# Retention and mLSTM: score-value products in plain fp32 instead of three fp32r matmuls on split operands

## The chip, the cores and the metric

The kernel runs on one core of one Trainium2 chip. The metric is the device time of one execution in microseconds; three runs of the kernel before gave 1383.99 (median), 1382.55 and 1386.01.

## The reference

A backbone of two layers works on 256 latent and 256 context tokens of width 1024. Layer 0 has a Mamba-2 (SSD) head group, four retention heads (query and key width 128, value width 256), an output projection and a SwiGLU FFN; layer 1 has an mLSTM block with four heads of width 512, its output projection and a second FFN; a last RMSNorm follows. The change touches one line of each mixer. In `decay_scan`, which retention uses:

```
scores = jnp.einsum('bihd,bjhd->bijh', qc, kc) * decay
y = (jnp.einsum('bijh,bjhe->bihe', scores, vc) + ...)
```

and in `mlstm_scan`:

```
s = jnp.einsum('bihd,bjhd->bijh', qc, kc) * jnp.exp(d - m_out[:, :, None, :])
num = (jnp.einsum('bijh,bjhe->bihe', s, vc) + ...)
```

The kernel computes both scans without chunks: all weighted scores of a head at once, forward and backward together, and then one product of scores and values.

## The kernel before, in words

All tokens stand side by side as 512 columns or four chunks of 128 rows. Each large product is done in split form: an fp32 operand is cast to a high part H of type fp32r, the rest L = x - H is kept in fp32r too, and `mm3` (L403) sums H·H, H·L and L·H in three fp32r matmuls (L407 to L409). Weights come through a list `plan` of 512 KB tiles: SP loads them (`wload`, L351), ScalarE casts wH (L367) and VectorE, for a few tiles named in `on_pool` POOL, subtracts wL (L368; the trace books every `tensor_tensor` on the helper's line L227).

Layer 0 takes its units in the order of `UNITS` (L378): R is a retention head, G an SSD group, O a quarter of the output projection. A retention head projects queries, keys, gate and values (`ret_proj`, L889); `projB` hands each of four 128 x 256 value blocks to `ev`, which copies it to vt (L905) and subtracts its low part vl (L906). `ret_scan` runs beside it as a background generator. It makes the decay matrix dm (L936), six score blocks in three PSUM tiles by plain fp32 matmuls (L945, L950), and hands each PSUM tile to `ret_split`: a product with dm on VectorE (L929), a cast on ScalarE (L931), a subtraction on POOL (L932), all of tiles named pT. Then come twelve pairs of a 128 x 128 score block and a 128 x 256 value block through `mm3` (L963), and the norm.

Layer 1 is driven by a string `order` (L1431): z is a tile of the z projection, c a step of the gate chain, h0 to h3 a step of a head's generator `ml_head` (L1312), d a tile of the down projection. A head's first step loads the decay rows ur (urow), splits its four value chunks into vH on ScalarE (L1319) and vL on POOL (L1320), and for each of two row blocks computes on VectorE and ScalarE the arguments of the exponentials (earg: L1329, L1331), their product with the scores (L1332), the divisor (rr) and the sum of both directions (L1342). The second step transposes the result on TensorE (L1349), copies it out of PSUM as pH (L1352) and subtracts pL on VectorE (L1353). The third makes eight pairs of a 128 x 128 block and a 128 x 512 value chunk through `mm3` (L1359) and the norm (L1362 to L1368); the fourth transposes back (L1376) and writes the operands of the down projection.

The tile framework allots the rotating buffers (tag s2: 36 of 2 KB per partition; tag s4: 8 of 4 KB), sets all semaphores and lays down, when the kernel is built, the order of each engine's instructions; SP alone keeps the order of the program. So the matmuls of a z tile can stand before and after a transpose of a head.

Of the kernel before, what the change touches and what calls it, by code (L numbers as in the profile page):

```python
# [17 lines left out]
P = 128  # L18
# [168 lines left out]
def tile_hybrid(ctx, tc, A, out, dbg=None):  # L187
# [35 lines left out]
    def f32v(t):  # L223
        return t.bitcast(F32)
# [664 lines left out]
    def ret_proj(h, pre=None):  # L889
        ready = {}  # L890
        bg.add(ret_scan(h, ready), True)

        def pa():
            p = projA(hs)
            slot()
            return p
        qk = ret_qk((pa, pa)) if pre is None else pre
        vt = pool[0].tile([P, NCH, 256], F32R, tag="s4", name=nm("vt"), bufs=8)
        gs = s4("gs")
        projB(hs, lambda c, p: S.activation(gs[:, c, :], p, AF.Silu))  # L900
        ready["qk"] = qk
        vl = [s2("vl", (P, 2, 256), F32R) for _ in range(2)]

        def ev(c, p):
            S.copy(out=vt[:, c, :], in_=p)  # L905
            tt(V, vl[c // 2][:, c % 2, :], p, f32v(vt)[:, c, :], ALU.subtract)  # L906
        projB(hs, ev)
        ready["vg"] = (vt, vl, gs)

    def ret_decay(h):  # L910

# [11 lines left out]
        tt(G, dm[:, 3, 128:256], ef[:, 0:128], eb[:, 384:512], ALU.add)  # L923
        return dm

    def ret_split(p, dm):

        t = s2("pT", (P, 2, 256))
        tt(V, t, p, dm, ALU.mult)  # L929
        H, L = (s2("pT", (P, 2, 256), F32R) for _ in range(2))  # L930
        S.copy(out=H, in_=t)  # L931
        tt(G, L, t, f32v(H), ALU.subtract)  # L932
        return [(H[:, j, :], L[:, j, :]) for j in range(2)]

    def ret_scan(h, ready):
        dm = ret_decay(h)  # L936
        yield
        while "qk" not in ready:
            yield
        q, k = ready["qk"]  # L940
        pt = []
        for jj in range(2):
            p = scps([P, 2, 256])
            for j in range(2):
                TE.matmul(p[:, j, :], lhsT=k[:, (jj * 2 + j) * P:(jj * 2 + j + 1) * P], rhs=q[:, LT_],  # L945
                          start=True, stop=True)
            pt += ret_split(p, dm[:, jj * 2:jj * 2 + 2, :])
        p = scps([P, 2, 256])
        for j in range(2):
            TE.matmul(p[:, j, :], lhsT=k[:, j * P:(j + 1) * P], rhs=q[:, CT_], start=True, stop=True)  # L950
        tc_ = ret_split(p, dm[:, 2:4, :])
        yield
        while "vg" not in ready:
            yield
        vt, vl, gs = ready["vg"]
        mv = small("mv", [P, NCH, 2], 2)
        rs = small("rsr", [P, NCH], 2)
        y = s4("yret")
        for st in range(2):
            py = scps([P, 2, 256])  # L960
            srcs = tc_ if st == 0 else pt
            for i in range(2):
                mm3(py[:, i, :], [(cols(src, slice(i * P, (i + 1) * P)), (vt[:, j, :], vl[j // 2][:, j % 2, :]))  # L963
                                  for j, src in enumerate(srcs)])
            sl = slice(st * 2, st * 2 + 2)
            for i in range(2):
                bs = small("bs", [P, 6], 2)
                V.bn_stats(out=bs, in_=py[:, i, :])
                V.bn_aggr(out=mv[:, st * 2 + i, :], in_=bs)
            V.tensor_scalar(out=rs[:, sl], in0=mv[:, sl, 1], scalar1=LN_EPS, scalar2=None, op0=ALU.add)  # L970
            tt(G, rs[:, sl], rs[:, sl], mhalf[:, :2], ALU.pow)
            for i in range(2):
                c = st * 2 + i
                V.scalar_tensor_tensor(out=y[:, c, :], in0=py[:, i, :], scalar=mv[:, c, 0:1], in1=gs[:, c, :],
                                       op0=ALU.subtract, op1=ALU.mult)
            for c in (st * 2, st * 2 + 1):
                S.activation(y[:, c, :], y[:, c, :], AF.Copy, scale=rs[:, c:c + 1])
            yield
        yield
        to_feat(y, (8 + 2 * h, 9 + 2 * h), (None, None))  # L980
        yield
# [330 lines left out]
    def ml_head(h):  # L1312
        ur = [s2x("urow") for _ in range(2)]
        for d in range(2):
            nc.sync.dma_start(out=ur[d], in_=scr2[d, h, :].partition_broadcast(P))
        vhl = []
        for c in range(NCH):
            H, L, v = s2("vH", dt=F32R), s2("vL", dt=F32R), vts[h][:, c, :]
            S.copy(out=H, in_=v)  # L1319
            tt(G, L, v, f32v(H), ALU.subtract)  # L1320
            vhl.append((H, L))
        pms = []
        for it in range(2):
            negm = small("negm", [P, 2], 2)
# [21 lines left out]
        for it in range(2):  # L1346
            pp = scps([P, NCH, P])
            for c in range(NCH):
                TE.transpose(pp[:, c, :], pms[it][:, c * P:(c + 1) * P], ident)  # L1349
            pp = pp.rearrange("p a b -> p (a b)")  # L1350
            H, L = s2("pH", dt=F32R), s2("pL", dt=F32R)
            S.copy(out=H, in_=pp)  # L1352
            tt(V, L, pp, f32v(H), ALU.subtract)  # L1353
            pts.append((H, L))
        yield
        ys = []
        for it in range(2):
            py = scps()
            mm3(py, [(cols(pts[it], slice(c * P, (c + 1) * P)), vhl[c]) for c in range(NCH)])  # L1359
            bs = small("bs", [P, 6], 2)  # L1360
            mv = small("mvm", [P, 2], 2)
            V.bn_stats(out=bs, in_=py)  # L1362
# [165 lines left out]
```

## Time and profile before

| | |
|---|---|
| median of three runs | 1383.99 us |
| the profiled execution | 1389.8 us, span 1388.0 us |
| granted TensorE clock, mean | 0.983 |
| TensorE busy | 1318.3 us (95%) |
| VectorE busy | 988.5 us (71%) |
| ScalarE busy | 661.1 us (48%) |
| POOL busy | 266.2 us (19%) |
| DMA | 200.73 MB, mean 145 GB/s |

Times are measured from the start of the span. In the rows PE is TensorE, PEld its weight load, DVE is VectorE, ACT is ScalarE. The matmuls' ends are modelled and overlap, so the pace of a series is read from the starts of its instructions. A plain fp32 matmul leaves two records, an fp32r matmul one. The row "xN" counts records.

### The profile page before, as it was taken

What the parts mean: (1) busy time and instruction counts of PE and PEld (TensorE: products, weight loads), DVE (VectorE), ACT (ScalarE), POOL (GpSimd) and SP (SyncE); (2) the same over time, 40 slices, a digit from 0 to 9 for tenths busy, and PEclk for the clock granted to TensorE, in tenths of its full rate; (3) what the DMA queues carried; (4) which work ended last, traced back from release to release, by engine and by line L of the source; (5) the groups of instructions that cost most, each with busy time, mean ns of one, the idle gap of its engine ahead of it and who ended that gap; (6) DMA issues with size and microseconds to landing.
All of it is one profiled execution on the core that took longest, in us unless ns stands there. A gap on an engine that the chain in (4) does not pass through costs nothing.

```text
span 1388.0 us, 21297 instructions
## 1 busy us (share of the span) xinstructions
PE 1318.3 (95%) x8238; PEld 1167.3 (84%) x8238; DVE 988.5 (71%) x1677; ACT 661.1 (48%) x1140; POOL 266.2 (19%) x214
## 2 busy tenths in 40 slices
PE   6898989999999999999999999989998979999997
PEld 2598867887899888888888888989998869999997
DVE  7987798785876668898557543676667998655555
ACT  4466646665754344221232133465666554544443
POOL 2235232342113131000000310421202341000001
PEclk9999999999999999999999999999999999999998
DMA  9245352634412224566547633311124334355553
GB/s 362 89 151 169 122 182 91 193 119 122 166 62 69 88 95 167 182 218 225 203 176 252 205 103 104 113 66 57 64 74 138 106 103 142 132 193 192 182 189 115
DMA packets 60839, 200.73 MB, mean 145 GB/s; under 512 B 6841, under 2 KB 8377, under 8 KB 60737
## 3 DMA queue, kind: packets, MB, share of 16 engines
q1 hardware_dynamic: 60594, 199.36, 41.9%
q8 instruction: 65, 1.06, 0.3%
q14 instruction: 36, 0.29, 0.1%
q10 hardware_dynamic: 144, 0.01, 0.0%
HBM read 197.16 MB, written 1.13 MB: 143 GB/s over the span
## 4 chain that ended last, share of the span: by engine, by line
PE 67%; DVE 10%; issue 5%; ACT 3%; DMA 2%; POOL 1%; POOLq 0%; SPq 0%; DVEq 0%; ACTq 0%
PE mm L407 20%; PE mm L408 20%; PE mm L409 20%; DVE conv L685 1%; DVE wL L227 1%; DVE junk L267 1%; ACT wH L367 1%; PE mm L1224 1%; DVE earg L1332 1%; DVE earg L1329 1%; PE sc L820 1%; DMA urow<-scr 1%; PE sc L838 1%; DMA erow<-scr 0%; DMA ada<-in_ada 0%
## 5 line engine op out<-in xcount | busy, mean ns | idle before, releaser
L367 ACT CAST wH<-wraw 128x1024 fp32r<-128x1024 f32 x248 | 258.7, 1047 | 413.8 <-PE mm L408 273.0
L227 DVE TENSOR_TENSOR wL<-wraw,wH 128x1024 fp32r<-128x1024 f32 x230 | 290.7, 1266 | 131.1 <-ACT wH L367 125.4
L409 PE MATMUL mm<-hH,wL 128*128 128x512 f32 (+1 forms) x568 | 218.9, 387 | 1.3 <-DVE wL L227 1.3
L408 PE MATMUL mm<-hL,wH 128*128 128x512 f32 (+1 forms) x568 | 219.3, 387 | 0.4 <-DVE hL L498 0.4
L407 PE MATMUL mm<-hH,wH 128*128 128x512 f32 (+1 forms) x568 | 217.9, 388 | 0.0
L267 DVE SCALAR_TENSOR_TENSOR junk<-ada,cbc 128x1024 bf16<-128x1024 f32 x128 | 167.8, 1311 | 18.4 <-DMA ada<-in_ada 17.3
L409 PEld LDWEIGHTS mm<-hH,wL 128*128 128x128 f32 x568 | 107.3, 189 | 25.4 <-DVE wL L227 1.8
L408 PEld LDWEIGHTS mm<-hL,wH 128*128 128x128 f32 x568 | 107.3, 189 | 23.9 <-DVE hL L498 0.6
L407 PEld LDWEIGHTS mm<-hH,wH 128*128 128x128 f32 x568 | 106.7, 189 | 23.0
L685 DVE SCALAR_TENSOR_TENSOR conv<-xp,prm,conv 128x512 f32<-128x512 f32 x128 | 107.5, 845 | 17.6 <-ACT conv L682 16.6
L988 DVE SCALAR_TENSOR_TENSOR xt<-mm,mod,xt 128x256 f32<-128x256 f32 x144 | 64.6, 479 | 67.2 <-PE mm L409 67.0
L407 PE MATMUL mm<-wH,hH 128*128 128x256 f32 x384 | 110.9, 289 | 0.1
L408 PE MATMUL mm<-hp,wH 128*128 128x256 f32 x384 | 109.1, 285 | 1.1 <-DVE hp L498 1.1
L408 PE MATMUL mm<-wL,hH 128*128 128x256 f32 x384 | 108.1, 282 | 1.7 <-DVE wL L227 1.7
L407 PE MATMUL mm<-hp,wH 128*128 128x256 f32 x384 | 109.0, 288 | 0.1
L409 PE MATMUL mm<-hp,wL 128*128 128x256 f32 x384 | 108.9, 285 | 0.0
L409 PE MATMUL mm<-wH,hL 128*128 128x256 f32 x384 | 107.7, 281 | 0.0
L407 PE MATMUL mm<-hHL,wH 128*128 128x256 f32 x352 | 99.5, 285 | 1.1 <-ACT hHL L497 1.1
L408 PE MATMUL mm<-hHL,wH 128*128 128x256 f32 x352 | 99.8, 284 | 0.0
L409 PE MATMUL mm<-hHL,wL 128*128 128x256 f32 x352 | 99.7, 283 | 0.0
L227 POOL TENSOR_TENSOR acc<-acc,sq 128x256 f32<-128x256 f32 (+1 forms) x23 | 25.0, 1086 | 277.2 <-ACT sq L453 276.9
L407 PEld LDWEIGHTS mm<-hp,wH 128*128 128x128 f32 x384 | 74.3, 195 | 3.1 <-ACT conv L682 2.0
(346 smaller groups left out, 3183.9 us busy)
## 6 DMA issues: line engine op xcount, KB each, us to landing
wraw<-in_f SPq DMA_DIRECT2D x136, 512.0 KB, 3.3
ada<-in_ada SPq DMA_DIRECT2D x80, 512.0 KB, 4.5
wraw<-in_win SPq DMA_DIRECT2D x48, 512.0 KB, 4.5
wraw<-in_wup SPq DMA_DIRECT2D x32, 512.0 KB, 3.2
erow<-scr SPq DMA_DIRECT2D x16, 512.0 KB, 6.5
wraw<-in_wout SPq DMA_DIRECT2D x16, 512.0 KB, 4.0
wraw<-in_wdn SPq DMA_DIRECT2D x16, 512.0 KB, 3.3
adaf<-in_ada SPq DMA_DIRECT2D x10, 512.0 KB, 7.4
```

Of the source, the lines that this page charges most:

```text
L227: eng.tensor_tensor(out=o, in0=a, in1=b, op=op)
L267: V.scalar_tensor_tensor(out=junk, in0=raw, scalar=1.0, in1=cbc[:, st, :], op0=ALU.mult, op1=ALU.mult, accum_out=mod[l][c][:, k, st:st + 1])
L367: S.copy(out=H, in_=raw)
L407: TE.matmul(o, lhsT=lh, rhs=rh, start=first and i == 0, stop=False)
L408: TE.matmul(o, lhsT=lh, rhs=rl, start=False, stop=False)
L409: TE.matmul(o, lhsT=ll, rhs=rh, start=False, stop=last and i == n - 1)
L685: V.scalar_tensor_tensor(out=o, in0=x[:, :, k:k + 256], scalar=pc(wname, t * 5 + k), in1=o, op0=ALU.mult, op1=ALU.add)
L820: TE.matmul(p[:, d, :], lhsT=btok[:, c, :], rhs=vws[n][:, d, :], start=True, stop=True)
L838: TE.matmul(p1[:, i, h * 64:(h + 1) * 64], lhsT=comb[(g, c0 + i)][:, h, :], rhs=xtok[:, c0 + i, h * 64:(h + 1) * 64], start=True, stop=True)
L988: V.scalar_tensor_tensor(out=xt[:, m, half], in0=p[:, o:o + 256], scalar=gate[:, m, st:st + 1], in1=xt[:, m, half], op0=ALU.mult, op1=ALU.add)
L1224: TE.matmul(pv[:, c, :], lhsT=xm[:, c0 // 2, 2 + c * P:2 + (c + 1) * P], rhs=b[:, P:], start=True, stop=True)
L1329: V.tensor_tensor_reduce(out=e, in0=ur[d], in1=mmask[it * 2 + d], scale=-1.0, scalar=0.0, op0=ALU.add, op1=ALU.min, accum_out=negm[:, d:d ...
```

## The change

The products of scores and values take their operands as plain fp32, in one matmul for each pair instead of three. `ret_proj` copies the values into an fp32 tile vt and makes no vl. `ret_split` becomes `ret_weigh`, which keeps only the product with dm. `ml_head` makes neither vH and vL nor pL; the transposed scores are copied out of PSUM as they are (pt). The order of units, the string `order` and the buffers' counts are the same.

```
-        vt = pool[0].tile([P, NCH, 256], F32R, tag="s4", name=nm("vt"), bufs=8)
+        vt = s4("vt")
...
-        vl = [s2("vl", (P, 2, 256), F32R) for _ in range(2)]
-
-        def ev(c, p):
-            S.copy(out=vt[:, c, :], in_=p)
-            tt(V, vl[c // 2][:, c % 2, :], p, f32v(vt)[:, c, :], ALU.subtract)
-        projB(hs, ev)
-        ready["vg"] = (vt, vl, gs)
+        projB(hs, lambda c, p: S.copy(out=vt[:, c, :], in_=p))
+        ready["vg"] = (vt, gs)
...
-    def ret_split(p, dm):
+    def ret_weigh(p, dm):
 
         t = s2("pT", (P, 2, 256))
         tt(V, t, p, dm, ALU.mult)
-        H, L = (s2("pT", (P, 2, 256), F32R) for _ in range(2))
-        S.copy(out=H, in_=t)
-        tt(G, L, t, f32v(H), ALU.subtract)
-        return [(H[:, j, :], L[:, j, :]) for j in range(2)]
+        return [t[:, j, :] for j in range(2)]
...
-                mm3(py[:, i, :], [(cols(src, slice(i * P, (i + 1) * P)), (vt[:, j, :], vl[j // 2][:, j % 2, :]))
-                                  for j, src in enumerate(srcs)])
+                for j, src in enumerate(srcs):
+                    TE.matmul(py[:, i, :], lhsT=src[:, i * P:(i + 1) * P], rhs=vt[:, j, :], start=j == 0,
+                              stop=j == len(srcs) - 1)
...
-        vhl = []
-        for c in range(NCH):
-            H, L, v = s2("vH", dt=F32R), s2("vL", dt=F32R), vts[h][:, c, :]
-            S.copy(out=H, in_=v)
-            tt(G, L, v, f32v(H), ALU.subtract)
-            vhl.append((H, L))
...
-            pp = pp.rearrange("p a b -> p (a b)")
-            H, L = s2("pH", dt=F32R), s2("pL", dt=F32R)
-            S.copy(out=H, in_=pp)
-            tt(V, L, pp, f32v(H), ALU.subtract)
-            pts.append((H, L))
+            pt = s2("pt", (P, NCH, P))
+            S.copy(out=pt, in_=pp)
+            pts.append(pt)
...
-            mm3(py, [(cols(pts[it], slice(c * P, (c + 1) * P)), vhl[c]) for c in range(NCH)])
+            for c in range(NCH):
+                TE.matmul(py, lhsT=pts[it][:, c, :], rhs=vts[h][:, c, :], start=c == 0, stop=c == NCH - 1)
```

## Rows read from the trace of the kernel before

**Rows 1.** The page's first part: busy time of each engine, its share of the span and its instructions.

```profile
PE 1318.3 (95%) x8238; PEld 1167.3 (84%) x8238; DVE 988.5 (71%) x1677; ACT 661.1 (48%) x1140; POOL 266.2 (19%) x214
```

**Rows 2.** Windows of the mLSTM head stage. Columns: stretch and its length, busy us of PE, PEld, DVE, ACT and POOL with records, granted clock, DMA share, GB/s.

```profile
1060.00:1080.00 20.00, 16.08 (x115) 15.42 (x115) 19.38 (x48) 15.24 (x30) 3.37 (x3) 0.91 0.38 133
1080.00:1100.00 20.00, 17.11 (x102) 15.54 (x101) 17.62 (x32) 9.13 (x17) 6.29 (x5) 0.91 0.51 164
1100.00:1120.00 20.00, 14.23 (x119) 13.82 (x117) 20.00 (x44) 12.76 (x27) 11.59 (x9) 0.95 0.13 47
1120.00:1140.00 20.00, 15.92 (x103) 14.74 (x104) 19.83 (x41) 10.53 (x19) 8.14 (x5) 0.88 0.24 82
```

**Rows 3.** Timeline of TensorE, mLSTM head stage, the instructions ahead of which it stood still for more than 1 us. Columns here and in all timelines: start us, length us, engine, line, operation, out<-in, shape, records, and in brackets the idle time before and what ended it.

```profile
1070.02 0.81 PE L1349 MATMUL sc<-cst,earg 128*128 128x128 f32 x4 [3.92 <-DVE rr L227]
...
1087.05 0.77 PE L1349 MATMUL sc<-cst,earg 128*128 128x128 f32 x4 [2.89 <-DVE rr L227]
...
1113.03 0.63 PE L1349 MATMUL sc<-cst,earg 128*128 128x128 f32 x4 [1.49 <-DVE earg L1342]
...
1122.19 1.09 PE L1349 MATMUL sc<-cst,earg 128*128 128x128 f32 x4 [6.47 <-DVE rr L227]
...
1129.77 0.50 PE L407 MATMUL sc<-vH,pH 128*128 128x512 f32 x1 [1.89 <-DVE pL L227]
```

**Rows 4.** Timeline of TensorE in layer 0: the first and the last of 47 fp32r matmuls of 256 columns, and behind them the plain fp32 matmuls of 256 columns of a retention head's scores (two records each).

```profile
441.10 0.28 PE L408 MATMUL mm<-wL,hH 128*128 128x256 f32 x1
...
446.52 0.28 PE L409 MATMUL mm<-wH,hL 128*128 128x256 f32 x1
446.63 1.89 PE L945 MATMUL sc<-qT,qT 128*128 128x256 f32 x8
448.36 1.03 PE L950 MATMUL sc<-qT,qT 128*128 128x256 f32 x4
```

**Rows 5.** Timeline of TensorE: the first and the last of the 24 fp32r matmuls of 512 columns of mLSTM head 0.

```profile
1077.12 0.40 PE L407 MATMUL sc<-vH,pH 128*128 128x512 f32 x1
...
1082.36 0.39 PE L409 MATMUL sc<-vH,pL 128*128 128x512 f32 x1
```

**Rows 6.** Answers by tile (vl, vH, pL, vL): one kind of instruction each, its count, the shortest, median and longest in ns, first and last start in us. The counts of L408 and L407 are those of the pairs.

```profile
L408 PE MATMUL sc<-vl,pT x48: 280/280/389, 96.8 to 466.1; 128*128 128x256 f32 x48
...
L407 PE MATMUL sc<-vH,pH x32: 389/389/497, 1077.1 to 1149.8; 128*128 128x512 f32 x32
...
L227 DVE TENSOR_TENSOR pL<-sc,pH x8: 677/680/692, 1072.4 to 1144.3; 128x512 fp32r<-128x512 f32 x8
...
L227 POOL TENSOR_TENSOR vL<-v,vH x16: 1297/1514/2272, 1053.0 to 1123.6; 128x512 fp32r<-128x512 f32 x16
```

**Rows 7.** Groups of VectorE's instructions from 1056 to 1130 us. Columns: line, engine, operation, out<-in, shape, count, busy us, mean ns, idle before.

```profile
L1332 DVE SCALAR_TENSOR_TENSOR earg<-earg,S 128x512 f32<-128x512 f32 x16 | 16.1, 1008 | 0.0
L227 DVE TENSOR_TENSOR wL<-wraw,wH 128x1024 fp32r<-128x1024 f32 x10 | 15.0, 1495 | 5.4 <-ACT wH L367 5.4
L1329 DVE CUSTOM_DVE_ANT_0 earg<-urow,mmask 128x512 f32<-128x512 f32 x16 | 14.6, 927 | 1.3 <-DMA urow<-scr 1.3
L1342 DVE SCALAR_TENSOR_TENSOR earg<-earg,rr,earg 128x512 f32<-128x512 f32 x7 | 7.2, 1028 | 0.0
L227 DVE TENSOR_TENSOR pL<-sc,pH 128x512 fp32r<-128x512 f32 x5 | 3.3, 682 | 0.6 <-ACT pH L1352 0.6
```

**Rows 8.** Timeline of VectorE: single instructions of these groups.

```profile
1058.09 1.48 DVE L1329 CUSTOM_DVE_ANT_0 earg<-urow,mmask 128x512 f32<-128x512 f32 x1 [0.22 <-DMA urow<-scr]
...
1059.49 2.87 DVE L1329 CUSTOM_DVE_ANT_0 earg<-urow,mmask 128x512 f32<-128x512 f32 x1
...
1097.89 0.69 DVE L1329 CUSTOM_DVE_ANT_0 earg<-urow,mmask 128x512 f32<-128x512 f32 x1 [1.12 <-DMA urow<-scr]
...
1122.64 0.68 DVE L1332 SCALAR_TENSOR_TENSOR earg<-earg,S 128x512 f32<-128x512 f32 x1
...
1123.33 1.21 DVE L227 TENSOR_TENSOR wL<-wraw,wH 128x1024 fp32r<-128x1024 f32 x1
...
1126.32 2.78 DVE L1332 SCALAR_TENSOR_TENSOR earg<-earg,S 128x512 f32<-128x512 f32 x1
...
1129.64 0.74 DVE L1342 SCALAR_TENSOR_TENSOR earg<-earg,rr,earg 128x512 f32<-128x512 f32 x1
```

**Rows 9.** Timeline of POOL in the same stage.

```profile
1058.97 2.84 POOL L227 TENSOR_TENSOR wL<-wraw,wH 128x1024 fp32r<-128x1024 f32 x1
...
1108.66 7.06 POOL L227 TENSOR_TENSOR vL<-v,vH 128x512 fp32r<-128x512 f32 x4 [3.45 <-ACT vH L1319]
...
1125.84 2.71 POOL L227 TENSOR_TENSOR wL<-wraw,wH 128x1024 fp32r<-128x1024 f32 x1
```

**Rows 10.** Timeline of TensorE behind the wait that ended at 1087.05: the first and the last of 14 fp32r matmuls of 256 columns.

```profile
1087.83 0.41 PE L408 MATMUL mm<-hp,wH 128*128 128x256 f32 x1
...
1090.61 0.38 PE L409 MATMUL mm<-hp,wL 128*128 128x256 f32 x1
```

**Rows 11.** Timelines in layer 0: VectorE's dt chain beside the first retention head, and two waits of TensorE.

```profile
90.63 2.26 DVE L512 SCALAR_TENSOR_TENSOR dt<-dt,dtlr 128x128 f32<-128x128 f32 x2
...
107.75 1.03 PE L660 MATMUL sc<-cst,cs 128*32 128x128 f32 x4 [3.61 <-DVE cs L650]
...
187.48 2.05 PE L820 MATMUL sc<-vw,btok 128*128 128x256 f32 x4 [5.89 <-DVE vw L227]
```

More of the change, by code (lines that the diff above doesn't have):

```diff
@@ L946, in ret_scan @@
                           start=True, stop=True)
-            pt += ret_split(p, dm[:, jj * 2:jj * 2 + 2, :])
+            pt += ret_weigh(p, dm[:, jj * 2:jj * 2 + 2, :])
         p = scps([P, 2, 256])
@@ L950, in ret_scan @@
             TE.matmul(p[:, j, :], lhsT=k[:, j * P:(j + 1) * P], rhs=q[:, CT_], start=True, stop=True)
-        tc_ = ret_split(p, dm[:, 2:4, :])
+        tc_ = ret_weigh(p, dm[:, 2:4, :])
         yield
@@ L954, in ret_scan @@
             yield
-        vt, vl, gs = ready["vg"]
+        vt, gs = ready["vg"]
         mv = small("mv", [P, NCH, 2], 2)
```

## The prediction

> **What bounds the kernel now.** I read the views from coarse to fine. The page first: TensorE is busy for 1318.3 of 1388.0 us and VectorE for 988.5 [rows 1]. Most of the span is therefore matmul after matmul, and there a change of the matmuls' own cost goes straight to the end. An average says nothing of the stages with the edited lines, so next come the windows. In the mLSTM head stage, 1060 to 1140 us, TensorE is busy for only 16.08 + 17.11 + 14.23 + 15.92 = 63.3 of 80 us, while VectorE is busy for 76.8 and in one window for all 20.00, and the granted clock is 0.88 to 0.95 [rows 2]. There VectorE sets the pace and TensorE waits. Retention lies elsewhere, among projections that fill TensorE.
>
> The timeline of TensorE shows the waits. Five times it stands still: 3.92, 2.89, 1.49 and 6.47 us ahead of the transposes of L1349 and 1.89 us ahead of the first product of L1359, each ended by VectorE [rows 3]. The last four sum to 12.7 us.
>
> **TensorE's price of the change.** A pair of score block and value chunk was three fp32r matmuls and becomes one plain fp32 matmul. For 256 columns, 47 fp32r matmuls start from 441.10 to 446.52, so one takes 5.42/46 = 0.118 us and three take 0.353; the kernel already has plain fp32 products of that shape: four at L945 start at 446.63 and L950 follows at 448.36, so one takes 1.73/4 = 0.4325 [rows 4]. The plain one is dearer by 0.079 us. Retention has 48 such pairs over four heads [rows 6]: 3.8 us, 0.95 a head.
>
> For 512 columns, 24 fp32r matmuls start from 1077.12 to 1082.36: 5.24/23 = 0.228 each, 0.683 for three [rows 5]. No plain 512-column product stands here warm. A lower bound is no extra at all, 0.683 (a row would have to show a plain product cheaper than its three parts, and L945 speaks against it); an upper one is four fp32r passes, 0.911, since the plain 256-column product lasts 0.4325/0.118 = 3.7 of them. I take twice the 256-column row, 0.865, because it is the same operation and only its columns are doubled: 0.182 more a pair. The mLSTM has 32 pairs [rows 6]: 5.8 us, between 0 and 7.3.
>
> The Trainium skill, page "FP8 and Floating Point Precision", section "TensorE Precision Notes", says that true fp32 takes four passes of high and low halves through the array; that speaks against this change, since the kernel ran three by hand. By it, at the fp32r pace, the 256-column product would take 0.471 us where the row shows 0.4325, and the 32 mLSTM pairs would cost 7.3 us more instead of 5.8.
>
> **What leaves the other engines.** In the mLSTM head: four casts vH on ScalarE, four subtractions vL on POOL, and two subtractions pL on VectorE, 0.68 us each; over four heads 16 vL of about 1.5 us and 8 pL [rows 6]. The copies out of PSUM stay (pH becomes pt; vt is still copied), so ScalarE loses only the casts vH and those of L931. Retention loses three casts, three POOL subtractions and four VectorE subtractions vl a head.
>
> The POOL work is worth more than its own time, since POOL is never the bound here: VectorE's instructions are stretched while it runs. From 1056 to 1130 us, 16 instructions of L1332 take 16.1 us, 16 of L1329 take 14.6, 7 of L1342 take 7.2 and 10 subtractions wL take 15.0 [rows 7]. Undisturbed, one takes 0.68, 0.69, 0.74 and 1.21 us [rows 8]. The excess is 5.2 + 3.6 + 2.0 + 2.9 = 13.7 us. The POOL timeline has vL through the same stretches, four of them from 1108.66 for 7.06 us; two wL on POOL, at 1058.97 and 1125.84, are no part of the change [rows 9]. Beside these two one L1329 takes 2.87 us and one L1332 2.78 [rows 8]: 2.2 + 2.1 = 4.3 us that stay. That leaves 9.4 us of stretching that goes with vL, and 3.3 us of pL in the same window [rows 7]: VectorE gets 12.7 us back.
>
> **What that does to the waits.** 12.7 us given back on the engine that ends the last four waits, against 12.7 us of such waits. TensorE also arrives later at each one, by eight dearer products, 1.5 us, for every head that has passed. So I take all four waits as gone: -12.7 us. I leave the first, 3.92 us, in: it comes at the start of the chain, and beside it lies only the end of head 0's vL, which stretches one L1329 to 1.48 us [rows 8]. Bounds: -6.4 if half comes back, -13.5 with that 0.8 us of the first. The change adds no wait: each product waits for one tile instead of two. What is late next would be the scores' copy out of PSUM on ScalarE, the new pt; it has no subtraction behind it any more and comes one instruction earlier than before.
>
> After the 2.89 us wait TensorE runs at the lower of its two levels, 1.2 GHz, the mean granted clock of that window being 0.91 [rows 2]: 14 matmuls from 1087.83 to 1090.61 are 2.78/13 = 0.214 us apart instead of 0.118 [rows 10]. That is 1.3 us which goes with the wait. For the longer wait of 6.47 us I take the same again: -2.6 together, between 0 and 4.
>
> **Retention.** Heads 2 and 3 lie where TensorE is nearly filled: +1.9 us, taken whole. In head 0, the subtractions pT on POOL stretch VectorE's small chain for dt (two L512 take 2.26 us), and TensorE later waits 3.61 us for cs, which that chain may shorten [rows 11]. But at 187.48 TensorE waits 5.89 us for a VectorE product [rows 11] behind loads of decay rows, and that can swallow a gain or a loss of the first two heads. I enter heads 0 and 1 at nothing, between 1.9 us lost (if that cover is gone) and 3.61 - 1.9 = 1.7 us gained.
>
> **Sum.** -12.7 - 2.6 + 5.8 + 1.9 = -7.6 us. The sum is made on the profiled execution of 1389.8 us, which then becomes 1382.2; that execution is 5.8 us above the median of 1384.0, from which the forecast is 1384.0 - 7.6 = **1376.4 us**.
>
> **The rivals.**
> 1. *Slower: TensorE pays and its waits return.* The order of each engine's instructions is laid down when the kernel is built. With shorter chains on the other engines, the transposes of L1349 can be put earlier between the z matmuls, and TensorE waits there as long as before. Then only the price is left: 5.8 + 3.8 = +9.6 us, 1393.6. The 9.6 us hold heads 0 and 1 too; the sign turns once less goes of the 15.3 us of waits and slow clock than the 7.7 us that the mLSTM and heads 2 and 3 pay. For it: the waits stand ahead of the very instructions that this order places. Against it: they are as long as the stretching by POOL, which no order brings back once vL is gone.
> 2. *No change.* Half of the waits and of the clock's loss returns, because a head's chain is also paced by its transfers of decay rows and by exponentials on ScalarE: -6.4 - 1.3 + 7.7 = 0, so 1384.0. For it: VectorE waits at 1097.89 for the transfer urow [rows 8].
> 3. *More.* The first wait shrinks too and the gain of retention's head 0 reaches the end: -7.6 - 0.8 - 1.7 = -10.1, 1373.9. It is the lower end of my own case rather than another.
>
> That the change doesn't do what it says I give nothing: plain fp32 tiles go through TensorE already.
>
> **How the numbers follow.** Forecast with rival 3: 0.57, between 1371 and 1380. No change: 0.26, 1380 to 1388. Slower: 0.17, 1388 to 1395. A difference of 0.3%, 4.2 us, is about what a measurement of this kernel can tell from none. Faster by more than that is my own case, 0.57 (its edge at 1380 is the line); within it 0.26; slower 0.17. The range is to leave out 2 in 10: it reaches from 1369 (rival 3, with half of the mLSTM's price, 2.9 us, and 1.4 us more of the clock) to 1391, half-way into the slower case.
>
> **What the new profile would show.** Right: plain products at L1359's place 0.86 us apart and at L963's place 0.43 apart, two records each; L1329, L1332 and L1342 near 0.7 us throughout but beside the two POOL wL; TensorE busy for over 18 of each 20 us in the head stage; no wait for VectorE above 1 us ahead of L1349 after the first. Wrong: waits of 3 us or more there again, then rival 1 or 2; a 512-column product far from 0.865; or a new long wait in layer 0 because the order there was laid out differently, which would be none of my steps.

## The result, and the profile after

The changed kernel takes 1364.53 us (median of 4 runs, 1364.11 to 1364.92) beside 1383.27 us for the kernel before (4 runs): a ratio of 0.9849, 95% interval 0.9816 to 0.9882. That is 18.7 us less where 7.6 were forecast, and below the range of 1369 to 1391.

The page's first part, as in [rows 1]:

```profile
PE 1315.0 (96%) x8158; PEld 1150.2 (84%) x8158; DVE 960.6 (70%) x1653; ACT 643.1 (47%) x1110; POOL 221.5 (16%) x186
```

TensorE is busy almost as long as before; the time came out of its waits, and out of stretches at the lower clock. Where it came from is read at two landmarks of TensorE's timeline: the end of layer 0's mixer (the first product of the norm's sum, L425, behind it) and the mLSTM head stage (from the cumulative gate product, L1284 before and L1277 after, to the next L425). The last FFN is left out: its code is the same in all kernels here, and it took 188 to 190 us in twelve of the profiled executions and 195 to 196 us in the other six, the kernel before's among them. The three instructions that mark the stages, first before, then after:

```profile
505.05 0.39 PE L425 MATMUL sc<-ones,acc 128*128 128x1 f32 x3
...
1047.10 0.59 PE L1284 MATMUL sc<-lf,cst 128*128 128x16 f32 x4 [0.64 <-DVE lf L1278]
...
1181.98 0.50 PE L425 MATMUL sc<-ones,acc 128*128 128x1 f32 x4
```

```profile
496.22 0.39 PE L425 MATMUL sc<-ones,acc 128*128 128x1 f32 x3
...
1038.12 0.59 PE L1277 MATMUL sc<-lf,cst 128*128 128x16 f32 x4 [0.65 <-DVE lf L1271]
...
1162.32 0.50 PE L425 MATMUL sc<-ones,acc 128*128 128x1 f32 x4
```

Layer 0's mixer ends 8.8 us earlier. The head stage lasts 134.9 us before and 124.2 after; 1.2 us of that are lost again in the norm behind it, whose transposes (L439) come at 1186.64 and at 1168.19 us.

**The mLSTM.** Windows of the head stage of the changed kernel, beside [rows 2]:

```profile
1060.00:1080.00 20.00, 19.48 (x121) 15.09 (x122) 18.19 (x45) 12.91 (x27) 1.10 (x2) 1.00 0.34 107
1080.00:1100.00 20.00, 19.73 (x127) 15.70 (x126) 18.81 (x56) 12.47 (x26) 1.77 (x2) 1.00 0.41 132
1100.00:1120.00 20.00, 17.35 (x103) 13.04 (x104) 19.22 (x41) 11.41 (x22) 3.79 (x3) 1.00 0.25 80
1120.00:1140.00 20.00, 20.00 (x131) 16.17 (x130) 12.72 (x24) 5.83 (x9) 3.48 (x3) 1.00 0.37 127
```

TensorE is busy for 76.6 of 80 us instead of 63.3, at a granted clock of 1.00 in every window. Its timeline shows what is left of the waits of [rows 3] (L1336 is before's L1349, L1345 before's L1359), and the pace of the plain products: eight of 512 columns, 16 records, in 7.03 us.

```profile
1060.30 0.63 PE L1336 MATMUL sc<-cst,earg 128*128 128x128 f32 x4 [3.19 <-DVE rr L227]
...
1080.90 7.03 PE L1345 MATMUL sc<-v,pt 128*128 128x512 f32 x16
...
1099.94 0.63 PE L1336 MATMUL sc<-cst,earg 128*128 128x128 f32 x4 [0.27 <-DVE rr L227]
...
1102.70 7.13 PE L1345 MATMUL sc<-v,pt 128*128 128x512 f32 x16 [1.02 <-ACT pt L1338]
...
1112.14 0.63 PE L1336 MATMUL sc<-cst,earg 128*128 128x128 f32 x4 [1.63 <-DVE yo L1366]
```

VectorE's groups from 1046 to 1115 us, which answer to [rows 7] (L1319 is before's L1332, L1316 before's L1329, L1329 before's L1342):

```profile
L1316 DVE CUSTOM_DVE_ANT_0 earg<-urow,mmask 128x512 f32<-128x512 f32 x16 | 12.2, 777 | 1.3 <-DMA urow<-scr 1.3
L1319 DVE SCALAR_TENSOR_TENSOR earg<-earg,S 128x512 f32<-128x512 f32 x16 | 10.6, 678 | 0.0
L1329 DVE SCALAR_TENSOR_TENSOR earg<-earg,rr,earg 128x512 f32<-128x512 f32 x8 | 6.0, 745 | 0.0
```

The means fell from 1008 to 678, from 927 to 777 and from 1028 to 745 ns: the same instructions, no longer stretched, but for one L1316 of 2.24 us beside a wL that POOL still does.

**Layer 0.** TensorE's waits between 60 us and the end of layer 0's mixer: line, what was waited for, us in total, times, longest. First the kernel before, then the changed one.

```profile
PE sc L820 <- DVE vw L227: 7.5, 2, 5.9
PE sc L660 <- DVE cs L650: 3.6, 1, 3.6
PE mm L408 <- DVE wL L227: 1.7, 1, 1.7
PE sc L734 <- ACT yssd L864: 1.4, 1, 1.4
```

```profile
PE sc L820 <- DVE vw L227: 5.3, 3, 2.6
PE sc L734 <- ACT yssd L864: 1.2, 1, 1.2
```

With the smaller ones the waits up to the mixer's end sum to 16.4 and 7.5 us. The first wait at L820 was 5.89 us [rows 11]; after, in the timelines of TensorE and VectorE:

```profile
179.37 1.10 PE L820 MATMUL sc<-vw,btok 128*128 128x256 f32 x4 [2.34 <-DVE vw L227]
180.82 1.97 PE L820 MATMUL sc<-vw,btok 128*128 128x256 f32 x8 [0.35 <-DVE vw L227]
...
178.38 1.18 DVE L227 TENSOR_TENSOR vw<-xtok,wdec 128x256 f32<-128x256 f32 x2
```

The window around it, before and then after (columns as in [rows 2]):

```profile
180.00:200.00 20.00, 14.11 (x50) 11.03 (x49) 18.48 (x38) 8.65 (x20) 6.77 (x4) 0.83 0.51 159
```

```profile
180.00:200.00 20.00, 19.65 (x104) 16.58 (x103) 18.47 (x36) 8.78 (x22) 8.30 (x5) 1.00 0.47 172
```

Behind the long wait TensorE ran part of the time at 1.2 GHz, the lower of its two levels (granted clock 0.83 in this window): the products of L820 held it from 187.48 to 192.37 us, 4.9 us; after, at 1.00, from 179.37 to 182.44, 3.1 us with the wait of 0.35 in it.

### The profile page after: what moved, and what is told of

Its sections match the earlier page's. It is cut to its first block, busy times and chain, and to the rows that moved or that the text cites. A ratio compares the mean times of both kernels' runs of the same rounds, so it can differ in the third digit from the quotient of the medians.

```text
span 1362.9 us, 21033 instructions
## 1 busy us (share of the span) xinstructions
PE 1315.0 (96%) x8158; PEld 1150.2 (84%) x8158; DVE 960.6 (70%) x1653; ACT 643.1 (47%) x1110; POOL 221.5 (16%) x186
## 4 chain that ended last, share of the span: by engine, by line
PE 77%; DVE 9%; issue 6%; ACT 3%; DMA 2%; POOL 1%; POOLq 0%; SPq 0%; DVEq 0%; ACTq 0%
PE mm L407 23%; PE mm L408 23%; PE mm L409 23%; DVE wL L227 1%; DMA erow<-scr 1%; PE mm L1217 1%; PE sc L1345 1%; PE sc L838 1%; PE sc L956 1%; DVE junk L267 1%; DVE conv L685 1%; ACT wH L367 1%; PE sc L820 1%; POOL wL L227 1%; DVE earg L1316 1%
## 5 line engine op out<-in xcount | busy, mean ns | idle before, releaser
L408 PE MATMUL mm<-hL,wH 128*128 128x512 f32 (+1 forms) x568 | 220.2, 388 | 0.4 <-DVE hL L498 0.4
L407 PE MATMUL mm<-hH,wH 128*128 128x512 f32 (+1 forms) x568 | 218.4, 389 | 0.0
L267 DVE SCALAR_TENSOR_TENSOR junk<-ada,cbc 128x1024 bf16<-128x1024 f32 x128 | 164.6, 1286 | 17.4 <-DMA ada<-in_ada 16.1
L408 PEld LDWEIGHTS mm<-hL,wH 128*128 128x128 f32 x568 | 107.8, 190 | 24.1 <-DVE hL L498 0.6
L407 PEld LDWEIGHTS mm<-hH,wH 128*128 128x128 f32 x568 | 106.7, 189 | 23.3
L407 PE MATMUL mm<-wH,hH 128*128 128x256 f32 x384 | 110.8, 289 | 0.0
L408 PE MATMUL mm<-hp,wH 128*128 128x256 f32 x384 | 107.8, 282 | 1.1 <-DVE hp L498 1.1
L407 PE MATMUL mm<-hp,wH 128*128 128x256 f32 x384 | 108.1, 286 | 0.0
L408 PE MATMUL mm<-wL,hH 128*128 128x256 f32 x384 | 108.0, 282 | 0.0
L407 PE MATMUL mm<-hHL,wH 128*128 128x256 f32 x352 | 97.8, 280 | 1.1 <-ACT hHL L497 1.1
L408 PE MATMUL mm<-hHL,wH 128*128 128x256 f32 x352 | 98.1, 279 | 0.0
L407 PEld LDWEIGHTS mm<-hp,wH 128*128 128x128 f32 x384 | 72.9, 192 | 3.2 <-ACT conv L682 2.0
L408 PEld LDWEIGHTS mm<-hp,wH 128*128 128x128 f32 x384 | 73.6, 192 | 1.9 <-DVE hp L498 1.3
```

The source lines that it names most:

```text
L267: V.scalar_tensor_tensor(out=junk, in0=raw, scalar=1.0, in1=cbc[:, st, :], op0=ALU.mult, op1=ALU.mult, accum_out=mod[l][c][:, k, st:st + 1])
L407: TE.matmul(o, lhsT=lh, rhs=rh, start=first and i == 0, stop=False)
L408: TE.matmul(o, lhsT=lh, rhs=rl, start=False, stop=False)
```

## The experiments

Four sets of runs; the kernel before measured 1384.34 us beside e1 to e4, 1382.65 beside a0, e5, e8 and e9, 1384.46 beside e6, e7, e10 and e11, and 1383.38 beside e12 to e15. The ratios are to it. The last two columns are the landmarks above, in us, from the one profiled execution of each.

| kernel | median us | ratio, 95% interval | layer 0's mixer ends | head stage lasts |
|---|---|---|---|---|
| before | 1383.27 | | 505.1 | 134.9 |
| after | 1364.53 | 0.9849 [0.9816, 0.9882] | 496.2 | 124.2 |
| a0, after again | 1370.88 | 0.9896 [0.9849, 0.9943] | 494.2 | 123.9 |
| e1, retention alone | 1374.38 | 0.9923 [0.9894, 0.9953] | 497.1 | 132.7 |
| e2, mLSTM alone | 1376.33 | 0.9933 [0.9901, 0.9965] | 506.1 | 125.7 |
| e3, POOL work kept, retention | 1373.02 | 0.9919 [0.9893, 0.9944] | 502.0 | 125.6 |
| e8, its control | 1365.38 | 0.9874 [0.9831, 0.9917] | 494.8 | 125.6 |
| e4, POOL work kept, mLSTM | 1379.44 | 0.9969 [0.9938, 1.0000] | 495.7 | 137.6 |
| e9, its control | 1365.08 | 0.9876 [0.9835, 0.9918] | 494.6 | 124.0 |
| e6, vl's work kept | 1378.63 | 0.9952 [0.9929, 0.9975] | 502.5 | 124.2 |
| e5, three passes | 1362.03 | 0.9851 [0.9810, 0.9892] | 498.0 | 119.1 |
| e11, heads 2 and 3 split | 1370.30 | 0.9896 [0.9866, 0.9927] | 493.6 | 125.6 |
| e7, before, pT's low part on VectorE | 1383.61 | 0.9990 [0.9965, 1.0014] | 501.8 | 135.1 |
| e12, before, ada products halved | 1383.34 | 0.9995 [0.9967, 1.0023] | 502.7 | 136.9 |
| e13, before, decay rows' own queue | 1384.78 | 1.0006 [0.9984, 1.0028] | 505.1 | 134.3 |
| e14, after, more VectorE work | 1369.59 | 0.9908 [0.9882, 0.9935] | 500.7 | 124.0 |
| e10, after, no wL on POOL | 1355.09 | 0.9801 [0.9763, 0.9839] | 491.8 | 120.9 |
| e15, before, no wL on POOL | 1379.14 | 0.9951 [0.9925, 0.9977] | 500.1 | 128.8 |

The runs of one kernel spread by 10 us (a0: 1362.02 to 1371.81) and more and its medians by 6 (a0 against after), so the stages tell more than the medians. Between kernels with the same or nearly the same code in a stage the landmarks spread too: 494.2 to 496.2 us for the end of layer 0 (after, a0, e4, e8, e9), 123.9 to 125.7 for the head stage (after, a0, e2, e3, e6, e8, e9, e11, e14), and 134.3 to 136.9 for that of the kernel before (before, e7, e12, e13).

**e1 and e2: one half each.** e1 has the new `ret_proj`, `ret_weigh` and `ret_scan` in the kernel before, e2 the new `ml_head`.

> The retention half of the change alone; the mLSTM heads split their operands as before. Theory (the halves are worth what the two traces show up to 1047 us and behind it): some 9 us faster than the kernel before, about 1374.5. By the terms on record (retention +1.9) it would be 1385; a rival on which the halves only work together gives anything near 1384.

> The mLSTM half alone; retention splits as before. Theory: -12.7 - 2.6 + 5.8 = -9.5, about 1374; if the mLSTM gain hung on a head stage that starts earlier, less, 1378 or more.

e1 came out as expected, e2 2 us above its 1374, and the stages agree: retention alone gives 505.1 - 497.1 = 8.0 us in layer 0 and little in the head stage, the mLSTM alone 134.9 - 125.7 = 9.2 us there and nothing in layer 0. The halves add up. The forecast had +1.9 us for the first of them.

**e3, e4 and their controls e8, e9: POOL's time.** e3 and e4 put the POOL subtractions' time back, results unused; e8 and e9 do so with 2 columns of 512.

```
         tt(V, t, p, dm, ALU.mult)
+        tt(G, s2("pD", (P, 2, 256)), t, t, ALU.subtract)
...
+        for c in range(NCH):
+            tt(G, s2("vD"), vts[h][:, c, :], vts[h][:, c, :], ALU.subtract)
```

> The changed kernel, but retention keeps one 128x512 POOL subtraction for each weighted score tile (12 in all, into a tile that nobody reads); no cast, no low part, plain products. Theory A (POOL's time beside VectorE was what retention paid for): most of the 9 us of layer 0 come back, 1371 or more. Rival B (VectorE's own vl, 6.7 us of work, or ScalarE's casts): 1 to 2 us back at most, 1365 to 1367. Rival C (the order laid down when the kernel is built): any change, and the same size whatever POOL does.

> The changed kernel, but each mLSTM head keeps four 128x512 POOL subtractions on its value chunks (16 in all, into tiles that nobody reads). Theory A: the stretching of VectorE returns, 9.4 us of the 12.7, and with it most of the waits: 1371 to 1375. Rival B (the gain was VectorE's pL and ScalarE's casts): 1365 to 1367.

> The control to e3: the same extra POOL subtraction behind each weighted score tile of retention (12 in all), at the same place in the program and with the same waits, but of 2 columns instead of 512. Theory (POOL's time beside VectorE's work is what costs): layer 0's mixer ends at 496 to 498 us as in the changed kernel, and the run takes 1364 to 1367 us. Rival (an instruction more in the lists lays the order out differently): 502 us and 1371 to 1373 us, as in e3.

> The control to e4: the same four extra POOL subtractions a head in the mLSTM (16 in all), of 2 columns instead of 512. Theory (POOL's time beside VectorE's work is what costs): the head stage lasts 124 to 126 us and the run takes 1364 to 1367 us. Rival (the order laid out differently by the extra instructions): 137 us and about 1378 us, as in e4.

> The changed kernel itself, as the yardstick of the runs beside it on this chip: 1365 us (1363 to 1367); layer 0's mixer ends at about 496 us and the mLSTM head stage, from the cumulative gate product of L1284 to the following norm product, lasts about 124 us.

a0's time, 1370.88 us, missed its 1363 to 1367; its stages came as expected. The full subtractions cost 502.0 - 494.8 = 7.2 us in layer 0 and 137.6 - 124.0 = 13.6 us in the head stage; of 2 columns they cost nothing there. So the loss of e3 and e4 is POOL's time and no shift in the order of instructions, and rival 1 falls with it. With POOL kept busy the dearer products are paid and the waits stay: e4 takes 1379.44 us, beyond the 1371 to 1375 expected, and its head stage is 2.7 us longer than that of the kernel before, with two waits of 6.2 and 6.1 us at L1338, the transposes. VectorE beside the four POOL instructions, first e4 and then e9, POOL's own rows last (L1318 is the line of L1316 above):

```profile
1053.75 1.52 DVE L1318 CUSTOM_DVE_ANT_0 earg<-urow,mmask 128x512 f32<-128x512 f32 x1
...
1055.20 1.52 DVE L1318 CUSTOM_DVE_ANT_0 earg<-urow,mmask 128x512 f32<-128x512 f32 x1
...
1053.23 5.83 POOL L227 TENSOR_TENSOR vD<-v 128x512 f32<-128x512 f32 x4
```

```profile
1051.62 0.68 DVE L1318 CUSTOM_DVE_ANT_0 earg<-urow,mmask 128x512 f32<-128x512 f32 x1
...
1052.23 0.68 DVE L1318 CUSTOM_DVE_ANT_0 earg<-urow,mmask 128x512 f32<-128x512 f32 x1
...
1051.10 2.48 POOL L227 TENSOR_TENSOR vD<-v 128x2 f32<-128x2 f32 x4
```

A POOL subtraction took 5.83/4 = 1.46 us, and each VectorE instruction beside one 1.52 us instead of 0.68. The vD at 1017.68 us in e4, with VectorE idle beside it, took 1.04 us: side by side both are held, and they go one for one. In e9 the four POOL instructions of 2 columns stretch nothing. An instruction of VectorE with one input in PSUM kept its time. In the kernel before, the product of scores and dm took 0.69 us wholly beside a POOL subtraction, as it did without one (0.69 at 88.58 us); VectorE's row first:

```profile
90.03 0.69 DVE L227 TENSOR_TENSOR pT<-sc,dm 128x512 f32<-128x512 f32 x1
...
90.00 1.29 POOL L227 TENSOR_TENSOR pT<-pT,pT 128x512 fp32r<-128x512 f32 x1 [11.19 <-ACT pT L931]
```

The Trainium skill, page "SBUF — State Buffer", section "Who interferes with whom", says that VectorE and GpSimd (POOL) share a pair of ports as an exclusive lock, and that a VectorE instruction with two inputs in SBUF contends with a GpSimd instruction that reads there, while one with a single SBUF input does not, outside VectorE's two-port modes; the rows of e4 and of the kernel before agree.

**e6: VectorE's own share.** The size and place of vl, results unused.

```
+        vd = [s2("vd", (P, 2, 256)) for _ in range(2)]
...
+            tt(V, vd[c // 2][:, c % 2, :], p, vt[:, c, :], ALU.subtract)
```

> The changed kernel with one extra VectorE subtraction behind each of the four value copies of a retention head (16 in all, 128x256, of the size and place of the removed low parts vl; the results are not used). Theory (the VectorE time of vl, ahead of the loads of decay rows, is the other part of what layer 0 gained): layer 0's mixer ends at 497 to 500 us instead of 494 to 496, the wait ahead of the first product of L820 is above 3.5 us. Rival (only POOL's time counts, VectorE has room in retention): 494 to 496 us and the wait at 2.3 to 3.3 us.

Layer 0 ends at 502.5 us, later than even the theory had it, with a first wait of 4.03 us at L820. Sixteen instructions of 0.42 us on VectorE cost as much as the twelve subtractions on POOL. Either alone takes back most of what layer 0 gained.

**e5: the price alone.** Three fp32r products again, on rounded operands without low parts.

```
...
-                for j, src in enumerate(srcs):
-                    TE.matmul(py[:, i, :], lhsT=src[:, i * P:(i + 1) * P], rhs=vt[:, j, :], start=j == 0,
-                              stop=j == len(srcs) - 1)
+                mm3(py[:, i, :], [((src[:, i * P:(i + 1) * P],) * 2, (vt[:, j, :],) * 2) for j, src in enumerate(srcs)])
...
+            mm3(py, [((pts[it][:, c, :],) * 2, (vts[h][:, c, :],) * 2) for c in range(NCH)])
```

> The changed kernel, but each pair of scores and values is three fp32r matmuls again, on operands rounded to fp32r, with the operand itself in the place of its low part: no low part is computed, nothing is added on the other engines. Theory (the price of plain fp32 stands whole on the path, 5.8 + 3.8 us): 1355 us; layer 0's mixer ends 3.8 us earlier than in the changed kernel (492.4 instead of 496.2) and the mLSTM head stage lasts 118.4 instead of 124.2 us. Rival (the price is hidden behind other waits, so the pure gain of the other engines is smaller than it seems): within 3 us of the changed kernel, 1362 to 1366, with the waits of TensorE longer by what the products are shorter.

Half right: 1362.03 us is what the rival had. The head stage lasts 119.1 us, 4.9 less than a0 and e9: the price stands there, nearly whole. In layer 0 it does not: the mixer ends at 498.0 us, 3 to 4 us later than in a0, e8 and e9, in spite of 3.8 us less of products. TensorE was earlier at L820 and waited there for 5.37 us, and the granted clock from 180 to 200 us was 0.83. So the price of heads 0 and 1 may have cost the change nothing, since without it TensorE comes early to a wait that VectorE ends. It is no clean test: vw also came later, at 180.36 us against 178.38 in the changed kernel, and why is not settled.

**e11: the price of heads 2 and 3.** There the old form is kept in the changed kernel (`split = h >= 2`).

> The changed kernel, but retention heads 2 and 3 keep the kernel before's three fp32r matmuls and low parts; heads 0 and 1 and the mLSTM are plain. Theory (in heads 2 and 3 TensorE is nearly filled, so 1.9 us of price come back): layer 0's mixer ends 1 to 2 us earlier than in the changed kernel, 493 to 495 us, and the run takes 1363 us. Rival (the POOL subtractions cost there what they cost in heads 0 and 1): layer 0 ends at 496 to 500 us and the run takes 1366 us or more.

493.6 us against 494.2 to 494.8: at most 1 us, less than the 1.9 expected and within the spread of this landmark, and 1370.30 us is no faster than a0. It is not told apart from nothing.

**e12, e13 and e14: what the wait at L820 is.** The prediction laid it to loads of decay rows. VectorE's timeline in the kernel before speaks against that: from 168.53 us on, the 27 rows ahead of vw have no idle time before them, and vw reads xtok and wdec, not a decay row. Some of them:

```profile
168.53 0.68 DVE L227 TENSOR_TENSOR yL<-sc,yH 128x512 fp32r<-128x512 f32 x1
...
171.06 1.22 DVE L267 SCALAR_TENSOR_TENSOR junk<-ada,cbc 128x1024 bf16<-128x1024 f32 x1
...
177.77 2.91 DVE L267 SCALAR_TENSOR_TENSOR junk<-ada,cbc 128x1024 bf16<-128x1024 f32 x1
...
184.83 1.37 DVE L267 SCALAR_TENSOR_TENSOR junk<-ada,cbc 128x1024 bf16<-128x1024 f32 x1
...
186.13 0.87 DVE L988 SCALAR_TENSOR_TENSOR xt<-mm,mod,xt 128x256 f32<-128x256 f32 x2
186.92 1.42 DVE L227 TENSOR_TENSOR vw<-xtok,wdec 128x256 f32<-128x256 f32 x4
```

```
+                w = D // 2 if (l, c, k) in ((0, 2, 7), (0, 3, 0), (0, 3, 1), (0, 3, 2)) else D
...
-            nc.sync.dma_start(
+            nc.scalar.dma_start(
                 out=e, in_=scr[c]
...
+        for n in range(4 if g == 0 else 0):
...
+            V.scalar_tensor_tensor(out=junk, in0=xtok.rearrange("p a b -> p (a b)"), scalar=1.0, in1=cbc[:, 0, :],
+                                   op0=ALU.mult, op1=ALU.mult, accum_out=small("dd", [P, 1], 2))
```

The first edit is e12's, the second e13's, the third e14's.

> The kernel before, with eight of VectorE's modulation products (L267) half as wide: those of the four ada tiles that lie between 171 and 186 us, ahead of the first product vw (half of their columns are left out of these sums). Theory V (VectorE, busy without a gap from 169 us on, is what the 5.89 us wait at L820 is made of): 8 x 0.6 = 4.8 us less ahead of vw, the wait falls to about 1 us, the clock stays up behind it, and layer 0's mixer ends 5 to 7 us earlier than in the kernel before, at 498 to 500 us. Rival (the wait is for something else, later by itself): under 2 us gained.

> The kernel before, with the loads of the decay rows (L747) issued from ScalarE's queue instead of SP's, so that they are not behind the ada and weight loads. Theory V (the wait at L820 is VectorE's queue of work): the rows land earlier and nothing moves; the wait ahead of L820 stays at 5 to 6 us and layer 0's mixer ends at 504 to 506 us. Rival L (the loads of decay rows on SP's queue hold the chain, as the prediction took it): the wait falls by several us and layer 0 ends at 500 us or earlier.

> The changed kernel with four more VectorE products of 128x1024 (1.2 us each, results not used) ahead of the products vw of the first SSD group. Theory V: vw comes 4.9 us later, the wait ahead of L820 grows from 2.3 to 2.9 us to about 7, the granted clock between 180 and 200 us falls as in the kernel before, and layer 0's mixer ends 5 to 7 us later, at 500 to 502 us. Rival (VectorE has slack there): under 2 us lost.

TensorE at the products of the first two SSD groups in e12 (L821 is L820 there):

```profile
183.83 4.51 PE L821 MATMUL sc<-vw,btok 128*128 128x256 f32 x12 [2.15 <-DVE vw L227]
...
264.22 1.19 PE L821 MATMUL sc<-vw,btok 128*128 128x256 f32 x2 [3.95 <-DVE vw L227]
```

The first wait falls from 5.89 to 2.15 us with VectorE's work, and L786, the transposes that open the second SSD group, is reached 5.7 us earlier (249.5 instead of 255.2). But the second group's wait for vw grows to 3.95 us, and layer 0's mixer ends 2.4 us earlier instead of 5 to 7; the run times show nothing of it.

VectorE and TensorE in e13, around the same wait:

```profile
187.19 1.23 DVE L267 SCALAR_TENSOR_TENSOR junk<-ada,cbc 128x1024 bf16<-128x1024 f32 x1 [4.61 <-DMA ada<-in_ada]
...
190.67 0.75 DVE L227 TENSOR_TENSOR vw<-xtok,wdec 128x256 f32<-128x256 f32 x2
...
191.23 1.19 PE L820 MATMUL sc<-vw,btok 128*128 128x256 f32 x2 [10.44 <-DVE vw L227]
```

The decay rows were issued at 174.34 us instead of 177.60, and the wait did not shrink: it grew to 10.44 us, where theory V had 5 to 6 and rival L several us less. The run also moved an ada load, for which VectorE now waited, so it does not price the loads of decay rows alone; against rival L speak the rows of the kernel before, where VectorE never stood still ahead of vw. The run shows something else: a delay of 3.7 us at L820 (191.23 against 187.48) had shrunk to 2.4 us at 294.9 (L734, the transposes of a finished SSD group, 297.3) and to 0.3 at 376.0 (L786), and at the end of layer 0 it was gone.

In e14 layer 0 ends at 500.7 us as expected, but not by the expected way. The extra products came to stand between the products vw and not ahead of the first, which starts at 178.61 us, as in the changed kernel (178.38); the last vw ended at 187.1 instead of 181.7 us. TensorE has two waits of 2.6 us at L820's place (L824) rather than one of 7, and a granted clock of 0.83 between 180 and 200 us:

```profile
179.59 0.67 PE L824 MATMUL sc<-vw,btok 128*128 128x256 f32 x2 [2.60 <-DVE vw L227]
183.54 1.22 PE L824 MATMUL sc<-vw,btok 128*128 128x256 f32 x2 [2.58 <-DVE vw L227]
```

**e7: the same move in the kernel before.** `tt(G, L, t, f32v(H), ALU.subtract)` of `ret_split` becomes `tt(V, ...)`.

> The kernel before, with the low parts of the weighted scores of retention (12 subtractions) on VectorE instead of POOL; the products stay three fp32r matmuls. Theory (POOL's time beside VectorE delays VectorE by more than the subtraction costs there): layer 0's mixer ends at 500 to 503 us instead of 505, the wait ahead of L820 is no longer than 5.9 us; the run takes 1378 to 1382 us. Rival (the work counts, not the engine): 12 x 0.7 = 8 us more on VectorE, layer 0 ends at 505 us or later and the run takes 1384 us or more.

501.8 us, as the theory had it, though VectorE got 12 subtractions more; the run times, 0.9990 [0.9965, 1.0014], do not show the 3.3 us, and the median, 1383.61, is outside the expected 1378 to 1382.

**e10 and e15: POOL's other subtractions.** If POOL's time is VectorE's time, the weight subtractions wL that POOL does are no gift either. There are 18 of them, as the rows below count; the expectations say 17.

```
-    on_pool = {nz + i for i in (-15, -13, -11, -8, -6, -3, 9, 19, 25)} | {12, 14, 15, 31, 43, 56, 70, 71, 74}
+    on_pool = set()
```

> The changed kernel with all 17 weight subtractions wL that POOL did moved to VectorE. Theory (each takes 1.21 us there, and beside it on POOL one VectorE instruction was stretched by about 1.6 us): no loss, 1362 to 1366 us; the mLSTM head stage lasts 122 to 125 us without the instructions of 2.2 to 2.9 us on VectorE. Rival (POOL carried this work for nothing): 17 x 1.2 = 20 us more on VectorE, of which a third lies where VectorE sets the pace: 1370 us or more.

> The kernel before with all 17 weight subtractions wL of POOL moved to VectorE, as e10 did with the changed kernel. Theory P (a subtraction on POOL costs VectorE more by stretching its instructions than it costs there): VectorE's busy time does not rise in spite of 17 more subtractions of 1.2 us, and the run takes 1374 to 1380 us. Rival (the gain of e10 needs the room that the change made): 1384 us or more.

First part of the page, e10 and then e15:

```profile
PE 1310.9 (97%) x8158; PEld 1148.2 (85%) x8158; DVE 956.2 (71%) x1671; ACT 644.0 (48%) x1110; POOL 176.2 (13%) x168
```

```profile
PE 1307.3 (96%) x8238; PEld 1156.4 (85%) x8238; DVE 987.1 (72%) x1695; ACT 661.4 (48%) x1140; POOL 219.1 (16%) x196
```

VectorE has 18 records more than in the changed kernel, and is busy for 4.4 us less: 956.2 against 960.6. Eighteen subtractions of 1.21 us are 21.8 us, so 26.2 us of stretching went, 1.5 us for each. e10 takes 1355.09 us, 0.9801 [0.9763, 0.9839], more than expected: the best version here. TensorE's first wait at L820 is down to 0.80 us, and the first wait of the head stage, which the forecast had left in, to 1.82:

```profile
1055.15 0.63 PE L1336 MATMUL sc<-cst,earg 128*128 128x128 f32 x4 [1.82 <-DVE earg L1329]
```

In the kernel before the same edit gives 4.2 us, at the edge of what was expected, and VectorE's busy time does not rise (987.1 against 988.5 us); layer 0 ends 5.0 us earlier and the head stage is 6.1 us shorter in the profiled execution, which was the fastest of the ten (1369.10 us).

## Why the prediction was wrong

**TensorE's price: right.** In the changed kernel the eight products at 1080.90 us are 16 records whose starts span 7.03 - 0.592 us (the last record's own length): 6.44/15 x 2 = 0.859 us a product, where 0.865 was taken. In retention 24 records at L956 take 5.34 us, 0.43 a product. The Trainium skill, page "FP8 and Floating Point Precision", section "TensorE Precision Notes", has four passes, which at the fp32r pace of [rows 5] is an estimate of 0.911. The trace agrees with the direction of that rule and stays below the estimate, at 3.8 times that pace. e5 gives the head stage's price as 4.9 us, 5.8 forecast.

```profile
452.29 5.34 PE L956 MATMUL sc<-vt,pT 128*128 128x256 f32 x24
```

**What VectorE gets back in the mLSTM: right.** e4 and e9 show that it is POOL's time. The four waits, 12.7 us, became 0.27 + 1.02 + 1.63 = 2.9; the forecast had them all gone. The first, 3.92, is 3.19. With the small ones, TensorE's waits up to the norm fall from 18.3 to 6.8 us, 11.5 less, of which the four are 9.8. The longest wait left behind the first is 1.63 us, for yo of VectorE; the scores' copy pt, which the prediction named as late next, comes second with 1.02 us. So two of the signs that it named fell short: a wait above 1 us, and one window of four with TensorE busy for 17.35 us instead of over 18.

**The clock there: low by 2.4 us.** From the gate product to L425 the stage is 10.7 us shorter. With 11.5 us of waits gone and 5.8 of price, 5.0 us are left for the clock, where 2.6 were entered, 4 at most. It is a remainder, not a measurement of its own; the windows show 1.00 where [rows 2] had 0.88 to 0.95. Part of it lies behind the first wait, for which no clock was entered: there 13 matmuls of 256 columns start 0.213 us apart from 1070.84 us on, and behind the 3.19 us that are left of that wait they start 0.12 us apart (from 1060.88).

Up to the norm's transposes, 139.54 us before and 130.07 after, the mLSTM came out at -9.5 us, forecast -12.7 - 2.6 + 5.8 = -9.5. That they agree this closely is luck: the waits gave 1.2 us less than entered, the clock 2.4 more, and 1.2 were lost in the norm.

**Retention: the step that failed.** The prediction wrote that at 187.48 us TensorE waits "for a VectorE product behind loads of decay rows, and that can swallow a gain or a loss of the first two heads. I enter heads 0 and 1 at nothing". Layer 0 measured -8.8 us instead of +1.9. The wait's length was read and the queue behind it was not: VectorE works without a gap for 18 us before vw, which reads no decay row, so the wait is VectorE's work, and work taken from VectorE earlier shortens it instead of vanishing in it. e12 shortens it to 2.15 us by taking VectorE's work away; with POOL's or vl's work put back into the changed kernel it is 5.2 us (e3) or 4.03 (e6) instead of 2.34. The gain was not swallowed: it is 4.6 us ahead of the wait (L786, the transposes that open the first SSD group, at 173.62 and 169.06), 10.3 us behind it (L838 at 201.3 and 191.0) and 8.8 at the mixer's end. The loss of the first two heads may have been swallowed, as the sentence said; e5 is in line with that, without settling it.

The second half of the same miss is that the reasoning used for the mLSTM, that a POOL subtraction takes its time from VectorE, was not carried to retention beyond the dt chain, because the average there said TensorE was filled. e3 and e6 give the two parts: POOL's 12 subtractions about 7 us, VectorE's 16 vl about as much, against a price of 3.8. Both act on the cs wait too: 3.61 us before, none after, 0.45 in e3, 2.02 in e6. By the views, 8.9 us less of waits, 2.2 us from the faster products of L820, and +3.8 us of price make -7.3; the other 1.5 us of the -8.8 are not placed. Two further stretches at the lower level nearly cancel: from 100 to 120 us, behind the cs wait, the granted clock was 0.91 before and is 1.00 after; from 250 to 270 us, where the second SSD group waits at L820, it was 1.00 and is 0.91.

**Heads 2 and 3: about half.** In the timelines the gain shrinks from 10.1 us (L734 at 294.9 before and 284.8 after) to 9.0 behind head 2 (316.1 and 307.1), about its 0.95, and stays at 8.8 behind head 3. There before had a wait of 0.57 us for pT ahead of L734, which went with the subtraction. e11 finds no more than 1 us, within the spread.

**The rivals.** Slower and no change: neither; the waits did not return, and the controls e8 and e9 show that more instructions in the lists do not bring them back. Rival 3, more, had the right sign: the cs wait of 3.61 us did vanish, and its gain did reach the end, but at 1373.9 it stopped 9 us short.

What stays open: the pieces of VectorE's work in layer 0 do not add up simply. e12 gains 5.7 us at 255 us and keeps 2.4, since the next wait for VectorE grew; e13's delay was gone by the end; and e3 and e6 together bring back more than the change gained. No run here prices a microsecond of VectorE there in general. Nor did one put back ScalarE's casts, vH and those of L931, so their share was not tested by itself.

## What to carry to other kernels

When a wait looks like cover, list the releasing engine's instructions ahead of it: if they have no gap, the wait is that engine's work, and work saved there can reach the end; how much of it does has to be measured. Price an offload to POOL by what VectorE's two-input instructions beside it lose, not by POOL's idle time; here each subtraction moved off VectorE cost VectorE more than it took there. And read which engine sets the pace in every stage that an edit touches, also where TensorE looks nearly filled.

## What the runs showed of the hardware

A short VectorE instruction can wait out the rest of a long POOL instruction. In the changed kernel rr, of 128x2 elements, took 2.31 us beside a wL on POOL, where the other seven in the head stage took 0.15 or 0.16. VectorE, then POOL:

```profile
1101.01 2.31 DVE L227 TENSOR_TENSOR rr<-rr,den 128x2 f32<-128x2 f32 x1
...
1100.59 2.71 POOL L227 TENSOR_TENSOR wL<-wraw,wH 128x1024 fp32r<-128x1024 f32 x1 [8.72 <-ACT wH L367]
```

It ended at 1103.32 us, the POOL instruction at 1103.30. So the price of this POOL subtraction was the rest of its own length, though the VectorE instruction that met it was of 128x2 elements. A POOL subtraction of 2 columns had no such price in e9.
